# Half of the weights' low parts added up by DMA instead of subtracted on VectorE

## The chip, the cores and the metric

The kernel runs on one core of one Trainium2 chip. The metric is the device time of one execution in microseconds, lower is better. The kernel before takes 2055.74 us (median of 2 runs, 2055.71 to 2055.78).

## The reference

One decoder layer on 256 tokens of width 2048, everything in float32: a gated mixer (differential attention, a causal convolution, chunkwise retention), cross-attention into 256 memory tokens, a SwiGLU, and norms between them. Nearly all of the arithmetic is products of a 256-token activation with weight matrices:

```python
proj = h @ w_in                                   # 2048 x 13312
merged = g0*(ya @ w_branch[0]) + g1*(yb @ w_branch[1]) + g2*(yr @ w_branch[2])
x = x + merged @ w_out                            # 2048 x 2048
...                                               # cross-attention: wq, wkv, wo
x = x + (silu(a) * b) @ w2                        # a, b = split(h @ w13), hidden 5632
```

## The kernel before, in words

Every weight matrix is stored in chunks of 512 rows by 512 columns (1 MB, four k-tiles of 128 rows). A block is 512 output columns; for it the kernel runs through the chunks of the inner dimension. One chunk is loaded by one DMA from SyncE's queue into a tile `raw` of 8 KB a partition. SyncE's loads keep their program order (`ld`, line 71).

A chunk is worked on in two halves of two k-tiles (128 partitions x 1024 elements). The precision of float32 is kept by splitting both operands: the high part is the number rounded to float32r, the low part is the number minus the high part. For each half, `emit_split` lets ScalarE round `raw` into `wh` (line 161), and then lets VectorE write `wl` = `raw` - `wh` (line 162). `products` issues 12 matmuls for a half: for each of two k-tiles and two token tiles high x high (line 178), high x low (line 179), low x high (line 180).

The main stream is a list of halves, and `emit_half` issues the splits `LA` halves ahead of the products. `wh` and `wl` rotate through `hlp` (4 buffers of each), `raw` through `rawp` (5 buffers). A buffer is taken again when its last reader is done: a `wh` or a `wl` when TensorE has finished the half, a `raw` when both engines have split both of its halves. The remaining work (rotary embedding, convolution, attention, norms, transposes) is made of generators which are advanced by one step after each half (`pump`), so that it falls between the halves. The order on each engine is set by the scheduler, which works out times for all instructions while the program is built; loads on SyncE are exempt.

GpSimd has little to do: the power of -0.5 of a few norm statistics (line 230) and 16 loads of 512 KB outside the weights, from its own, software-driven DMA queue (decay, memtok, memT, xtok again, gfin: lines 535, 319, 243, 786, 938).

Line numbers from line 163 on are 4 higher in the changed kernel: what is line 180 before is line 184 there.

Of the kernel before, what the change touches and what calls it, by code (L numbers as in the profile page):

```python
# [24 lines left out]

# columns of the packed parameter tile
_PC = {}
# [12 lines left out]

LA = 3


class Act:
    """Four k-tiles of a transposed activation, as exact high and low float32r parts."""

# [7 lines left out]
def trunk(ctx, tc, xT, xtok, memT, memtok, w_in, w_br, w_out, w_q, w_kv, w_o, w_13, w_2,  # L54
          prm, cst, decay, gfin, out):
    nc = tc.nc
    P = 128

    cpool = ctx.enter_context(tc.tile_pool(name="cpool", bufs=1))
    rawp = ctx.enter_context(tc.tile_pool(name="rawp", bufs=5))  # L60
    hlp = ctx.enter_context(tc.tile_pool(name="hlp", bufs=4))
    s4 = ctx.enter_context(tc.tile_pool(name="s4", bufs=28))
# [27 lines left out]

    # ---------------------------------------------------------------- background tasks
    active = []
# [22 lines left out]

    # ---------------------------------------------------------------- main stream
    items = []
    halves = []

    def half_jobs(psref, chunks, acts, start, stop, alloc=None, ts=(0, 1), keep=False):  # L120
        """Products of activation chunks with weight chunks into the block's two banks."""
        n = len(chunks)
        for i, (w, a) in enumerate(zip(chunks, acts)):
            for h in range(2):
                j = dict(ps=psref, src=w, h=h, act=a, start=start and i == 0 and h == 0,
                         stop=stop and i == n - 1 and h == 1, alloc=alloc or alloc_mm, ts=ts, keep=keep)
                halves.append(j)
                items.append(("half", len(halves) - 1))
# [17 lines left out]
    def emit_split(i, before=None):  # L146
        j = halves[i]
        while state["dma"] <= i // 2:
            emit_dma(state["dma"])
        r = raws[i // 2]  # L150
        rv = r[:, 2 * j["h"]:2 * j["h"] + 2, :]
        if j["keep"]:
            hi = S4([P, 2, 512], F32R)
            lo = S4([P, 2, 512], F32R)
        else:
            hi = hlp.tile([P, 2, 512], F32R, tag="wh", name=nm("wh"))
            lo = hlp.tile([P, 2, 512], F32R, tag="wl", name=nm("wl"))
        for sl in ((slice(0, 1), slice(1, 2)) if i == 0 else (slice(0, 2),)):
            if before is not None:
                before(sl.start)  # L160
            sc.copy(hi[:, sl, :], rv[:, sl, :])  # L161
            ve.tensor_tensor(out=lo[:, sl, :], in0=rv[:, sl, :], in1=hi[:, sl, :].bitcast(F32), op=ALU.subtract)  # L162
        j["hi"], j["lo"] = hi, lo
        if j["h"] == 1:
            raws.pop(i // 2)
# [36 lines left out]
    def block(W, nb, acts, evac):  # L202
        """One 512-column block; evac(ps) is called once its products are issued."""
        ps = []
        half_jobs(ps, [W[nb, c] for c in range(len(acts))], acts, True, True)
        call(lambda: evac(ps[2]))

    # ---------------------------------------------------------------- constants
    prm_t = cpool.tile([P, PCOLS], F32, name="prm_t")
# [16 lines left out]
    def rstd_of(dst, src, scale, w):  # L226
        """dst = (src*scale + eps) ** -0.5 on a few columns."""
        v = TN(w)
        ve.tensor_scalar(out=v, in0=src, scalar1=scale, scalar2=EPS, op0=ALU.mult, op1=ALU.add)
        nc.gpsimd.tensor_tensor(out=dst, in0=v, in1=nhalf[:, :w], op=ALU.pow)  # L230
# [8 lines left out]
    def load_actT(a, src, g, c):  # L239
        """Load a transposed chunk, times its gain, in parts."""  # L240
        def gen():
            r = S4([P, 4, 256])
            nc.gpsimd.dma_start(out=r, in_=src[c])
            yield
            for k in range(0, 4, 2):
                actT_part(a, r, g, c, (k, k + 1))
                yield
        return gen()
# [6 lines left out]
    def transposed(a, src, gain):  # L255
        """Transposed chunk in parts: src(kt, t) are [128, 128] blocks; gain(kt) or None."""
        def gen():
            a.hi = S4([P, 4, 256], F32R)
            a.lo = S4([P, 4, 256], F32R)
            for pr in range(2):  # L260
                tp = TP().rearrange("p (k c) -> p k c", k=2)
                for k in range(2):
                    for t in range(2):
                        nc.tensor.transpose(tp[:, k, t * P:(t + 1) * P], src(2 * pr + k, t), ident)  # L264
                yield
                if gain is None:
                    sl = slice(2 * pr, 2 * pr + 2)
                    sc.copy(a.hi[:, sl, :], tp)  # L268
                    ve.tensor_tensor(out=a.lo[:, sl, :], in0=tp, in1=a.hi[:, sl, :].bitcast(F32),  # L269
                                     op=ALU.subtract)  # L270
                else:
                    for k in range(2):
                        split_gain(a, 2 * pr + k, tp[:, k, :], gain(2 * pr + k))
                yield
        return gen()

    def transposed_f32(dst, src):
        """dst [128, 4, 256] plain float32 transposes of src(kt, t)."""
        for pr in range(2):
# [8 lines left out]
    def blk(tl):  # L288
        """tl [128, 2, 512] token-major -> accessor of its [128,128] blocks."""
        return lambda k, t: tl[:, t, k * P:(k + 1) * P]  # L290

    def sumsq(tl, dst):
        """dst[:, t] = sum over the block's 512 columns of the square."""
        junk = S4([P, 2, 512])
        for t in range(2):
            sc.activation(junk[:, t, :], tl[:, t, :], AF.Square, accum_out=dst[:, t:t + 1])  # L296

    # ---------------------------------------------------------------- start
    gmix = cpool.tile([P, 16], F32, name="gmix")
# [14 lines left out]
    def tok_stats(src, dst, eng):  # L314
        """rstd of a token-major input."""
        parts = cpool.tile([P, 4, 2], F32, name=nm("parts"))
# [10 lines left out]
    def start_task():  # L327
# [24 lines left out]
        sc.activation(le, l2, AF.Exp)  # L352
        # -(e0 - e1 + lambda_init)
        ve.tensor_tensor(out=lam_t, in0=le[:, 1:2], in1=le[:, 0:1], op=ALU.subtract)
# [5 lines left out]
    def prologue():  # L360
        # keeps TensorE busy, and so at its full clock, while the first loads arrive
        sc.copy(warm, nhalf[:, 0:1])
# [20 lines left out]
    def scaled(ps, rs, extra=None):  # L383
        """Token-major copy of a block times the tokens' rstd."""
        o = S4([P, 2, 512])
# [3 lines left out]

    # ---------------------------------------------------------------- conv branch  # L390
    cv = {}
# [103 lines left out]

    # ---------------------------------------------------------------- rope
    def ev_rope(store, key, half, ro):
        """Rotary embedding on a block's heads, then its transposes."""
        nh = 512 // (2 * half)
# [25 lines left out]

    # ---------------------------------------------------------------- retention
    yr = [Act(), Act()]
# [65 lines left out]

    # ---------------------------------------------------------------- differential attention
    ya = [Act(), Act()]
# [88 lines left out]

    # ---------------------------------------------------------------- gated merge
    merged = [None] * 4
# [34 lines left out]

    # ---------------------------------------------------------------- keys and values of the memory
    kM = [None] * 4
# [25 lines left out]

    # ---------------------------------------------------------------- w_out, residual  # L750
    def residual(W, acts, xin, aT, gname, rs, parts, order=None):
        """x + acts @ W; the sum's rstd and its gained transposes for the next stage."""
        xs = [None] * 4
# [42 lines left out]

    # ---------------------------------------------------------------- cross-attention
    oT = [Act() for _ in range(4)]
# [14 lines left out]
    def prep_kv(h):  # L813
        """Parts of a head's transposed keys and of its values."""
        def gen():
# [12 lines left out]
    def mm3(out, l, r, start, stop):  # L828
        """out += l.T @ r from the parts (lhsT, rhs) of l and r."""
        nc.tensor.matmul(out, l[0], r[0], start=start, stop=False)  # L830
# [72 lines left out]

    # ---------------------------------------------------------------- SwiGLU
    hT = [Act() for _ in range(11)]
# [44 lines left out]
    def finish(nb, t, p):  # L950
        """Residual of one token tile's block; after the last one its norm and the store."""
        r = x2[nb][:, t, :]
# [137 lines left out]
```

## Time and profile before

| | before |
|---|---|
| median of the runs | 2055.74 us |
| span of the profiled execution, first to last instruction | 2054.3 us |
| TensorE busy | 2042.2 us, 99% |
| VectorE busy | 1194.7 us, 58% |
| ScalarE busy | 959.8 us, 47% |
| GpSimd busy | 20.3 us, 1% |
| bytes moved by DMA | 390.33 MB, 190 GB/s over the span |

The profile shows one execution. Busy time of an engine is time in which it executes an instruction; matmuls overlap in the pipeline, so that their summed durations are larger than TensorE's busy time. The page gives no time of the profiled execution besides its span; the median of the runs, which are timed without a profile, is 1.4 us longer than it. The chain of waits follows the end of the program back to its beginning: 99% of it is TensorE.

### The profile page before, as it was taken

The numbers are of one execution on the slowest core, as the hardware profiler recorded it, in microseconds if no ns is written. First come the engines' busy times: TensorE is split into PE (matmuls) and PEld (weight loads), VectorE is DVE, ScalarE is ACT, GpSimd is POOL, SyncE is SP. The second block draws the span as 40 slices with busy tenths as digits, with TensorE's granted clock in tenths as the row PEclk, the third lists the DMA queues.
The fourth block names the chain that finished last, engine by engine and source line by source line (L and its number), as shares of the span: only waits on it lengthen the run. The fifth ranks groups of instructions, "written<-read, shape, count | busy, mean of one in ns | idle before, by whom it ended". The sixth has DMA issues, their size and how long they took to land.

```text
span 2054.3 us, 23424 instructions
## 1 busy us (share of the span) xinstructions
PE 2042.2 (99%) x9369; PEld 1689.4 (82%) x9369; DVE 1194.7 (58%) x1505; ACT 959.8 (47%) x1190; POOL 20.3 (1%) x32
## 2 busy tenths in 40 slices
PE   9999999999999999999999999999999999999998
PEld 6888888888888888888888888888888888888886
DVE  6995699776654557444455555544455444455445
ACT  7444444558444455444445554444444334444443
POOL 0000000000000000000000000000000000000000
PEclk9999999999999999999999999999999999999999
DMA  9555444444555655655555444555555556555552
GB/s 374 185 188 202 174 175 174 166 164 163 186 212 196 220 200 215 227 203 185 200 186 182 151 149 158 184 185 188 196 189 184 189 200 207 195 192 185 185 199 88
DMA packets 57277, 390.33 MB, mean 190 GB/s; under 512 B 6480, under 2 KB 6736, under 8 KB 11984
## 3 DMA queue, kind: packets, MB, share of 16 engines
q1 hardware_dynamic: 54720, 380.44, 51.6%
q0 software_dynamic: 2304, 8.39, 1.1%
q8 instruction: 73, 1.20, 0.2%
q14 instruction: 36, 0.29, 0.0%
q10 hardware_dynamic: 144, 0.01, 0.0%
HBM read 386.72 MB, written 2.10 MB: 189 GB/s over the span
## 4 chain that ended last, share of the span: by engine, by line
PE 99%; DMA 0%; issue 0%; DVE 0%; SPq 0%; ACTq 0%; ACT 0%; POOLq 0%; POOL 0%
PE mm L178 31%; PE mm L179 31%; PE mm L180 31%; PE tp L264 1%; PE tp L178 1%; PE tp L179 1%; PE tp L180 1%; PE tp L283 0%; PE tp L832 0%; PE tp L831 0%; PE tp L830 0%; DMA raw<-in_w_in 0%; PE tp L622 0%; PE tp L558 0%; PE tp L620 0%
## 5 line engine op out<-in xcount | busy, mean ns | idle before, releaser
L162 DVE TENSOR_TENSOR wl<-raw,wh 128x1024 fp32r<-128x1024 f32 (+1 forms) x705 | 860.8, 1222 | 780.8 <-ACT wh L161 780.3
L161 ACT CAST wh<-raw 128x1024 fp32r<-128x1024 f32 (+1 forms) x705 | 740.8, 1052 | 956.2 <-PE mm L180 909.8
L178 PE MATMUL mm<-wh,s 128*128 128x512 f32 x2752 | 1078.4, 392 | 1.6 <-ACT wh L161 1.6
L179 PE MATMUL mm<-wl,s 128*128 128x512 f32 x2752 | 1075.3, 391 | 1.2 <-DVE wl L162 1.2
L180 PE MATMUL mm<-wh,s 128*128 128x512 f32 x2752 | 1073.7, 390 | 0.0
L178 PEld LDWEIGHTS mm<-wh,s 128*128 128x128 f32 x2752 | 516.8, 188 | 109.4 <-ACT wh L161 3.3
L180 PEld LDWEIGHTS mm<-wh,s 128*128 128x128 f32 x2752 | 516.7, 188 | 107.8
L179 PEld LDWEIGHTS mm<-wl,s 128*128 128x128 f32 x2752 | 517.0, 188 | 106.9 <-DVE wl L162 2.4
L433 DVE SCALAR_TENSOR_TENSOR s<-s,prm_t,s 128x227 f32<-128x227 f32 (+29 forms) x240 | 98.2, 464 | 0.0
L264 PE MATMUL tp<-cst_t,s 128*128 128x128 f32 x280 | 42.7, 272 | 0.0
L264 PEld LDWEIGHTS tp<-cst_t,s 128*128 128x128 f32 x280 | 34.5, 140 | 7.9
L269 DVE TENSOR_TENSOR s<-tp,s 128x512 fp32r<-128x512 f32 x46 | 31.1, 682 | 0.0
L251 ACT ACTIVATE s<-tp,prm_t 128x256 fp32r<-128x256 f32 x40 | 18.6, 472 | 19.1 <-DVE s L252 16.8
L268 ACT CAST s<-tp 128x512 fp32r<-128x512 f32 x46 | 26.4, 582 | 0.5 <-PE tp L264 0.5
L178 PE MATMUL tp<-wh,s 128*128 128x512 f32 x64 | 24.9, 389 | 0.0
L179 PE MATMUL tp<-wl,s 128*128 128x512 f32 x64 | 24.9, 389 | 0.0
L180 PE MATMUL tp<-wh,s 128*128 128x512 f32 x64 | 24.9, 389 | 0.0
L252 DVE SCALAR_TENSOR_TENSOR s<-tp,prm_t,s 128x256 fp32r<-128x256 f32 x40 | 19.0, 480 | 9.1 <-ACT s L251 9.1
L913 ACT ACTIVATE s<-mm,rs 128x512 f32<-128x512 f32 x22 | 13.9, 686 | 16.7 <-PE mm L180 16.7
L694 ACT ACTIVATE s<-mm,rsx 128x512 f32<-128x512 f32 x24 | 15.2, 685 | 12.5 <-PE mm L180 12.4
L296 ACT ACTIVATE s<-s 128x512 f32<-128x512 f32 x32 | 19.9, 624 | 1.4 <-DVE s L758 1.4
L921 DVE SCALAR_TENSOR_TENSOR s<-mm,rs,s 128x512 f32<-128x512 f32 x22 | 15.5, 747 | 4.6 <-PE mm L180 4.6
(172 smaller groups left out, 682.2 us busy)
## 6 DMA issues: line engine op xcount, KB each, us to landing
raw<-in_w SPq DMA_DIRECT2D x132, 1024.0 KB, 4.8
raw<-in_w_in SPq DMA_DIRECT2D x117, 1024.0 KB, 4.8
raw<-in_w_kv SPq DMA_DIRECT2D x32, 1024.0 KB, 4.8
raw<-in_w_br SPq DMA_DIRECT2D x24, 1024.0 KB, 4.8
raw<-in_w_out SPq DMA_DIRECT2D x16, 1024.0 KB, 4.8
raw<-in_w_q SPq DMA_DIRECT2D x16, 1024.0 KB, 4.9
raw<-in_w_o SPq DMA_DIRECT2D x16, 1024.0 KB, 4.8
raw<-in_w_in SPq DMA_DIRECT2D x5, 512.0 KB, 9.3
```

What stands on the lines that cost most here:

```text
L161: sc.copy(hi[:, sl, :], rv[:, sl, :])
L162: ve.tensor_tensor(out=lo[:, sl, :], in0=rv[:, sl, :], in1=hi[:, sl, :].bitcast(F32), op=ALU.subtract)
L178: nc.tensor.matmul(ps[t], ah, hi[:, k, :], start=j["start"] and k == 0, stop=False)
L179: nc.tensor.matmul(ps[t], ah, lo[:, k, :], start=False, stop=False)
L180: nc.tensor.matmul(ps[t], al, hi[:, k, :], start=False, stop=stop and k == 1)
L251: sc.activation(a.hi[:, k, :], src, AF.Identity, scale=g)
L252: ve.scalar_tensor_tensor(out=a.lo[:, k, :], in0=src, scalar=g, in1=a.hi[:, k, :].bitcast(F32), op0=ALU.mult, op1=ALU.subtract)
L264: nc.tensor.transpose(tp[:, k, t * P:(t + 1) * P], src(2 * pr + k, t), ident)
L268: sc.copy(a.hi[:, sl, :], tp)
L269: ve.tensor_tensor(out=a.lo[:, sl, :], in0=tp, in1=a.hi[:, sl, :].bitcast(F32), op=ALU.subtract)
L296: sc.activation(junk[:, t, :], tl[:, t, :], AF.Square, accum_out=dst[:, t:t + 1])
L433: ve.scalar_tensor_tensor(out=o[:, s:], in0=uT[:, k, :T - s], scalar=pc("cw", c * CW + CW - 1 - s), in1=o[:, s:], op0=ALU.mult, op1=ALU.add)
```

## The change

Of each chunk from the fifth on (`i >= 8`), the second half gets its low part in another way. ScalarE rounds `raw` a second time, with the sign turned, straight into `wl`; a DMA from GpSimd's queue then reads the same weights from HBM once more and adds them to `wl` in SBUF. The first half of each chunk, the first four chunks and the last weights (`keep`) are split as before. The look-ahead goes from 3 halves to 4, `hlp` from 4 to 5 buffers, `rawp` from 5 to 4. The other lines of the diff drop comments and are left out here.

```diff
-LA = 3
+LA = 4
...
-    rawp = ctx.enter_context(tc.tile_pool(name="rawp", bufs=5))
-    hlp = ctx.enter_context(tc.tile_pool(name="hlp", bufs=4))
+    rawp = ctx.enter_context(tc.tile_pool(name="rawp", bufs=4))
+    hlp = ctx.enter_context(tc.tile_pool(name="hlp", bufs=5))
...
             sc.copy(hi[:, sl, :], rv[:, sl, :])
+            if i >= 8 and i % 2 == 1 and not j["keep"]:
+                sc.activation(lo, rv, AF.Identity, scale=-1.0)
+                nc.gpsimd.dma_start(out=lo, in_=j["src"][:, 2:4, :], accum_op=ALU.add)
+                continue
             ve.tensor_tensor(out=lo[:, sl, :], in0=rv[:, sl, :], in1=hi[:, sl, :].bitcast(F32), op=ALU.subtract)
```

In the whole program 348 half-chunks are changed: ScalarE has 348 instructions more (line 163), VectorE 348 fewer, GpSimd 348 DMAs more (line 164).

ScalarE in the input projection, before (`raw` is a chunk, `wh` the high part of a half):

```order
L161 CAST wh_767<-raw_765 128x1024
L161 CAST wh_785<-raw_765 128x1024
L161 CAST wh_805<-raw_803 128x1024
L161 CAST wh_825<-raw_803 128x1024
L161 CAST wh_846<-raw_844 128x1024
```

and in the changed kernel:

```order
L161 CAST wh_726<-raw_724 128x1024
L163 ACTIVATE wl_745<-raw_724 128x1024
L161 CAST wh_744<-raw_724 128x1024
L161 CAST wh_765<-raw_763 128x1024
L163 ACTIVATE wl_784<-raw_763 128x1024
L161 CAST wh_783<-raw_763 128x1024
```

Three instructions per chunk stand where two were, and the scheduler puts the negated copy of the second half ahead of that half's own rounding.

GpSimd at the second retention group, before (`tn` are statistics of a norm, `s` from `in_decay` is a load):

```order
L230 TENSOR_TENSOR rsx<-tn_428,nhalf 128x2
L535 DMA s_201_1333<-in_decay 128x1024
L230 TENSOR_TENSOR tn_1923<-tn_1924,nhalf 128x8
L535 DMA s_332_2112<-in_decay 128x1024
L230 TENSOR_TENSOR tn_2700<-tn_2701,nhalf 128x8
```

and in the changed kernel, the stretch that ends with the same second load:

```order
L164 DMA wl_1802<-in_w_in 128x1024
L164 DMA wl_1849<-in_w_in 128x1024
L234 TENSOR_TENSOR tn_1967<-tn_1968,nhalf 128x8
L164 DMA wl_1902<-in_w_in 128x1024
L164 DMA wl_1972<-in_w_in 128x1024
L164 DMA wl_2034<-in_w_in 128x1024
L164 DMA wl_2083<-in_w_in 128x1024
L164 DMA wl_2138<-in_w_in 128x1024
L539 DMA s_334_2158<-in_decay 128x1024
```

The powers of the norms and the loads, which had this queue to themselves, now stand between the adding DMAs.

## Rows read from the trace of the kernel before

**Rows 1.** The page's first part: engine, busy us (share of the span) xinstructions.

```profile
PE 2042.2 (99%) x9369; PEld 1689.4 (82%) x9369; DVE 1194.7 (58%) x1505; ACT 959.8 (47%) x1190; POOL 20.3 (1%) x32
```

**Rows 2.** Waits, last SyncE's queue: engine line <- waited for: us, times, longest us.

```profile
ACT wh L161 <- PE mm L180: 909.8, 574, 6.1
...
PE mm L178 <- ACT wh L161: 1.6, 3, 0.5
...
SPq L71 <- DVE wl L162: 1730.3, 329, 12.3
```

**Rows 3.** Timeline, 900 to 903 us: start us, us, engine, instruction [idle before <-releaser].

```profile
901.40 0.39 PE L180 MATMUL mm<-wh,s 128*128 128x512 f32 x1
...
901.63 0.39 PE L178 MATMUL mm<-wh,s 128*128 128x512 f32 x1
...
901.83 1.05 ACT L161 CAST wh<-raw 128x1024 fp32r<-128x1024 f32 x1 [1.67 <-PE mm L180]
901.85 0.39 PE L179 MATMUL mm<-wl,s 128*128 128x512 f32 x1
```

**Rows 4.** ScalarE's timeline over the end of a block, same columns.

```profile
1733.98 1.05 ACT L161 CAST wh<-raw 128x1024 fp32r<-128x1024 f32 x1 [1.67 <-PE mm L180]
1736.70 1.27 ACT L913 ACTIVATE s<-mm,rs 128x512 f32<-128x512 f32 x2 [1.67 <-PE mm L180]
1737.86 1.05 ACT L161 CAST wh<-raw 128x1024 fp32r<-128x1024 f32 x1
1739.42 1.05 ACT L161 CAST wh<-raw 128x1024 fp32r<-128x1024 f32 x1 [0.52 <-PE mm L180]
```

**Rows 5.** Groups by form: line engine op xcount | busy us, mean ns | idle before.

```profile
L162 DVE TENSOR_TENSOR wl<-raw,wh 128x1024 fp32r<-128x1024 f32 x703 | 859.4, 1224 | 777.8 <-ACT wh L161 777.3
L161 ACT CAST wh<-raw 128x1024 fp32r<-128x1024 f32 x703 | 739.5, 1053 | 953.2 <-PE mm L180 909.8 <-PE tp L180 13.5 <-DVE s L433 10.0
...
L913 ACT ACTIVATE s<-mm,rs 128x512 f32<-128x512 f32 x22 | 13.9, 686 | 16.7 <-PE mm L180 16.7
```

**Rows 6.** DMA queues: packets, MB, share of 16 engines; issues: KB, us to landing.

```profile
q1 hardware_dynamic: 54720, 380.44, 51.6%
q0 software_dynamic: 2304, 8.39, 1.1%
...
raw<-in_w SPq DMA_DIRECT2D x132, 1024.0 KB, 4.8
...
s<-in_memT POOLq DMA_DIRECT2D x4, 512.0 KB, 4.6
```

**Rows 7.** GpSimd's loads of `memT`, all four: time from issue to landing.

```profile
DMA to landing us min/median/max: 3.9/4.6/4.9
```

**Rows 8.** GpSimd's load of `decay` at 40.6 us: time from issue to landing.

```profile
DMA to landing us min/median/max: 9.1/9.1/9.1
```

**Rows 9.** Stretches: us, busy us of each engine, granted clock, DMA share, GB/s.

```profile
25.00:50.00 25.00, 25.00 (x112) 20.71 (x111) 14.21 (x24) 18.06 (x27) 1.35 (x2) 1.00 1.01 417
50.00:200.00 150.00, 150.00 (x679) 124.40 (x679) 121.01 (x200) 66.16 (x69) 0.00 (x0) 1.00 0.54 191
200.00:600.00 400.00, 400.00 (x1912) 329.74 (x1911) 295.10 (x535) 204.96 (x294) 8.50 (x7) 1.00 0.49 176
600.00:900.00 300.00, 300.00 (x1341) 248.79 (x1340) 162.76 (x151) 141.61 (x169) 6.51 (x12) 1.00 0.59 209
900.00:1000.00 100.00, 100.00 (x442) 82.78 (x442) 45.33 (x37) 44.12 (x48) 0.00 (x0) 1.00 0.54 191
1000.00:1400.00 400.00, 400.00 (x1928) 335.25 (x1927) 215.29 (x236) 196.03 (x267) 1.41 (x2) 1.00 0.49 175
1400.00:2000.00 600.00, 600.00 (x2686) 496.11 (x2684) 295.53 (x261) 249.65 (x256) 1.10 (x2) 1.00 0.54 192
```

**Rows 10.** GpSimd's timeline, three of its rows.

```profile
231.90 1.67 POOL L230 TENSOR_TENSOR tn<-tn,nhalf 128x8 f32<-128x8 f32 x1 [190.60 <-DVE tn L229]
...
769.32 1.10 POOL L243 DMA_DIRECT2D s<-in_memT  x2
...
841.13 1.05 POOL L786 DMA_DIRECT2D s<-in_xtok  x2 [61.45 <-PE mm L180]
```

## The prediction

> **What bounds the kernel now.** I read the page's first part, then who waited for whom, then a short timeline, then the DMA tables. TensorE is busy for 99% of the span, VectorE for 58%, ScalarE for 47% [rows 1]. The waits say which of them sets the pace: ScalarE's rounding waits 909.8 us for TensorE to give buffers back, TensorE waits 1.6 us for ScalarE, and SyncE's queue waits 1730.3 us for VectorE to free a `raw` [rows 2]. So everything runs ahead of TensorE and is held back by buffers; nothing but TensorE's own pace is on the path. That pace can be read off ScalarE's clockwork: a rounding every 2.72 us (1733.98, 1736.70), with 1.67 us of idle time ended by TensorE [rows 4]. A half has 12 matmuls, so one is issued every 0.227 us, and a chunk takes 5.44 us. TensorE idles 2054.3 - 2042.2 = 12 us in all, which is the most that any change off TensorE can give back: 0.6%.
>
> **What is removed.** 348 subtractions of 1.224 us on VectorE [rows 5], 426 us: VectorE goes from 1194.7 to about 769 us, 37%. Since TensorE did not wait for it, this is worth nothing.
>
> **What ScalarE gets.** 348 negated roundings of 128x1024 from SBUF. Their form is not in the trace. From below it is the rounding of the same shape, 1.05 us; from above two scaled activations of 128x512 from PSUM, 2 x 0.686 = 1.37 us [rows 5]. I take 1.2 us, between them: 418 us, so that ScalarE stands at 1378 us, 67%. In each chunk it has 2 x 1.05 + 1.2 = 3.3 us of 5.44, which leaves 2.1 us for the rest. At a block's end the eviction pushes a rounding back by 1737.86 - 1736.70 = 1.16 us, and the one after it is on time again [rows 4]. A block ends with a second half; with 5 buffers, what is freed then goes to a first half, so the pushed one is not the negated copy. I put ScalarE at nothing; its cover is the spare time below.
>
> **What the low part now waits for.** This is the term that decides. Before, three halves of lead are 8.2 us, of which rounding and subtraction take 2.3: 5.9 us to spare. Now the negated copy for half i starts when TensorE leaves half i-5. The timeline has that distance: the last matmul of a half starts at 901.40, the next half at 901.63, the freed rounding at 901.83, so 0.20 us into the half [rows 3]. `wl` is first read by the second matmul of half i, 0.23 us into it. From one to the other are 4 x 2.72 + 0.23 - 0.20 = 10.9 us; less 1.2 for the copy, **9.7 us are left for the adding DMA from issue to landing**.
>
> No adding DMA is in the trace. From below it is a plain load of the same 512 KB from the same queue: 3.9 us at the least, 4.6 at the median [rows 7]. From above I take two of the slowest in a row, one to read the weights and one to read what they are added to: 4.9 + 4.9 = 9.8 us. I choose 4.6 us and one more reading of 0.52 MB at the best rate shown, 417 GB/s [rows 9], 1.26 us: 5.9 us, because the additional half is a stream and not a second round from issue to landing. That leaves 3.8 us to spare, and no steady wait. If a landing takes L all the time, the four halves stretch until they hold it: each chunk grows by (L - 9.7) / 2, and 348 chunks by 174 us for each microsecond too many.
>
> **What the DMA engines get.** 348 x 0.524 MB = 182 MB beside 390 MB. A `raw` of 1.05 MB takes 2.5 us at 417 GB/s. With each added byte read once, a chunk needs 2.5 + 1.26 = 3.8 us of 5.44; with the destination read as well, 2.5 + 2.5 = 5.0 us. Both fit at that rate. The loads of `raw` keep their cover: a `raw` is freed about 2.5 us into half 2k-3, and the chunk that takes it, four later, is wanted at half 2k+4, so 7 x 2.72 - 2.5 = 16.5 us for a load that lands in 4.8 [rows 6]. One buffer fewer of `raw` therefore costs nothing, as long as the engines are not full.
>
> The Trainium skill's Collectives: The Full Stack (The bandwidth ceiling: the fold count and why AG ≠ RS ≠ AR) says that a reduction by DMA is half as fast as a copy, not because of the add but because both sources are read through the same ring. By that rule the second of the two figures holds, 5.0 us of 5.44, and my sum stays as it is, with little room; no row here has an adding DMA to test it.
>
> **Where small losses are.** (1) The start. From 25 to 50 us the DMA engines are full, 417 GB/s at a share of 1.01 [rows 9], and a 512 KB load issued there landed after 9.1 us [rows 8]. Five adding DMAs fall there (halves 9 to 17, from 26 us on, every 5.44 us). 9.1 + 1.26 = 10.4 us is 0.7 late, half of that per chunk: 2 us. They also bring 2.6 to 5.2 MB, 6 to 12.6 us of full engines, most of which displaces loads that are not urgent. I take 5 us in all, from 0 to 15. (2) GpSimd's queue. Its issues take 0.53 us (1.10 for two) and the powers 1.67 us [rows 10]; either fits into 3.8 us. The queue is in order, though: an adding DMA behind a power waits as long as that power waits for VectorE's statistics, and the four loads of `xtok` now stand in a row ahead of one, 4 x 1.26 = 5.0 us of transfer, 1.2 us too many. I take 3 us, from 0 to 40 (some 20 places at up to 2 us).
>
> **The sum.** -0 (VectorE) + 0 (ScalarE) + 5 (start) + 3 (GpSimd's queue) = +8 us on the profiled span of 2054.3; the median of the runs is 1.4 us above that span, so 2055.74 + 8 = **2064 us**. Its own range is 2050 to 2096: TensorE's idle time cannot give back more than a few us, and the upper end is that of GpSimd's queue, 40 us.
>
> **The rivals.** *The DMA engines are full.* For it: the share of busy engines, as the profile counts it, is much higher than the best rate suggests: 0.54 at 191 or 192 GB/s [rows 9]. If that share is work and not waiting, and an adding DMA costs two readings, then each byte of `raw` brings another of the same cost. Adding up the stretches in which the doubled share passes 1: 50 to 200 us 1.08, +12; 600 to 900 us, where 0.05 of the 0.59 are other loads, 1.13, +38; 900 to 1000, 1.08, +8; 1400 to 2000, 1.08, +48; the stretches with 0.49 stay under 1. Together 106 us and the 8 from above: 2170. If it costs three plain readings at 417 GB/s, a chunk takes 2.5 + 3.8 = 6.3 us against 5.67 (348 chunks in about 1975 us): +219, 2283. At four, 7.5 us and some 2720. It decides from 5.67 - 2.5 = 3.2 us of all 16 engines per adding DMA. Against it: 417 GB/s held for 25 us. Chance 0.33. The rule of the skill named above is this rival's two readings.
>
> *The landing is late, with engines to spare.* Reading, adding and writing back in turn, behind the other queue's packets, could take longer than 9.7 us everywhere. If the start's 10.4 us became the rule: 0.7 x 174 = 122 us, 2186; at 11 us, 2290. For it: 9.1 us has been seen for a plain load. Against it: only where the engines were full; 3.9 to 4.9 elsewhere. Chance 0.15. This one and the one before end on the slower side.
>
> *GpSimd's queue holds the adding DMAs up* at each power and load, 40 us: about 2100. Chance 0.05; against it speaks that VectorE, whose statistics are waited for, gets freer.
>
> *Faster by what VectorE gives up.* TensorE's idle time is 12 us in all [rows 1], far from 2%, so that it would have to issue its matmuls closer than every 0.227 us, for which nothing speaks. Chance 0.01.
>
> **How the numbers follow.** The forecast keeps 0.46: it is the likeliest single case, though the slower ones together hold more. A difference under about 2% is what two measurements of this kernel would call none (2015 to 2097 us). Faster 0.01, within 2% 0.46, slower 0.53 (0.33 + 0.15 + 0.05). The range goes from 2050 to 2350: it takes in the forecast, the full engines at two and three readings, late landings to about 11 us and the queue; what is left out is four readings and more, and later landings, some 0.2.
>
> **What would show it.** If right: TensorE's waits for `wl` stay at a few us outside the first 60 us, the adding DMAs land in 5 to 8 us, the DMA share is 0.75 to 0.95, ScalarE still waits for TensorE. If the engines are full: a share near 1 all along, `raw` landing much later than 4.8 us, ScalarE waiting for `raw`. If the landing is late: TensorE waiting at line 183 (the old 179) for the DMA once in each chunk, with a share well under 1. If the queue: long gaps on GpSimd ended by VectorE just before an adding DMA. My price of the adding DMA is the weakest step; all else rests on rows.

## The result, and the profile after

| | before | changed |
|---|---|---|
| median of the runs, 2 of each | 2055.74 us | 2135.8 us |
| ratio, with its 95% interval | | 1.0389 (1.0358 to 1.0419) |
| span of the profiled execution | 2054.3 us | 2136.0 us |

The change costs 80 us, 3.9%. The forecast of 2064 us was the likeliest single case and did not come; the time lies in the range, on the slower side that held 0.53.

The page's first part of the changed kernel, to be read against [rows 1]:

```profile
PE 2073.7 (97%) x9369; PEld 1688.4 (79%) x9369; DVE 781.1 (37%) x1157; ACT 1280.8 (60%) x1536; POOL 322.7 (15%) x380
```

VectorE moved about as worked out (769 us were expected), ScalarE by less (1378). TensorE has the same 9369 matmuls, but is idle for 62 us instead of 12, and busy for 31 us more: a matmul lasts 0.39 us and the next one starts after 0.23, so that a short wait between them shows no idle time, and a matmul that waits for its weights only a little shows as a longer one.

Who waited for whom, all engines (columns as in [rows 2]; line 183 is the old 179):

```profile
ACT wl L163 <- PE mm L183: 380.4, 294, 10.1
...
PEld mm L183 <- DMA wl<-in_w: 29.7, 35, 3.2
...
PE mm L183 <- DMA wl<-in_w: 15.5, 23, 2.8
...
PE mm L183 <- DMA wl<-in_w_out: 6.8, 1, 6.8
```

TensorE now waits at the matmul that first reads `wl`, and for a DMA. ScalarE still waits for TensorE, so it isn't the bound. The DMA part of the page, against [rows 6]:

```profile
q0 software_dynamic: 52416, 190.86, 49.5%
q1 hardware_dynamic: 54720, 380.44, 46.8%
...
raw<-in_w SPq DMA_DIRECT2D x132, 1024.0 KB, 9.5
...
wl<-in_w POOLq DMA_DIRECT2D x128, 512.0 KB, 10.0
```

Both queues together take 96% of the engines' time by the profile's count; before it was 53%. A `raw` lands after 9.5 us instead of 4.8. The adding DMAs (line 164), all 348:

```profile
DMA to landing us min/median/max: 5.5/9.8/19.4
```

The timeline around two of them (columns as in [rows 3]):

```profile
1497.67 0.87 POOL L164 DMA_DIRECT2D wl<-in_w  x1 [4.81 <-ACT wl L163]
...
1501.93 1.06 ACT L163 ACTIVATE wl<-raw 128x1024 fp32r<-128x1024 f32 x1 [1.40 <-PE mm L183]
1501.96 0.39 PE L182 MATMUL mm<-wh,s 128*128 128x512 f32 x1
...
1503.29 0.87 POOL L164 DMA_DIRECT2D wl<-in_w  x1 [4.75 <-ACT wl L163]
...
1503.95 0.33 SPq L71 DMA_DIRECT2D raw<-in_w  x1
...
1507.40 0.39 PE L182 MATMUL mm<-wh,s 128*128 128x512 f32 x1
1507.76 0.19 PEld L183 LDWEIGHTS mm<-wl,s 128*128 128x128 f32 x1 [0.39 <-DMA wl<-in_w]
1507.76 0.50 PE L183 MATMUL mm<-wl,s 128*128 128x512 f32 x1
```

Two things are to be seen. The first matmul on `wl` (1507.76) starts 0.36 us after the one before it, where 0.23 is the pace. It waits for the adding DMA of 1497.67, some 10 us before, which is late by a hair. This does not happen in every chunk. From 1400 to 2000 us, inside the SwiGLU, 105 adding DMAs are issued, and the waits of TensorE's weight loads for them in that stretch are 29 (us, times, longest us):

```profile
PEld mm L183 <- DMA wl<-in_w: 22.3, 29, 1.5
```

And the load of the next `raw` is issued 0.66 us after the adding DMA (1503.95 against 1503.29), so that the two share the engines nearly from beginning to end. Four stretches, against [rows 9]:

```profile
25.00:50.00 25.00, 23.23 (x103) 18.91 (x102) 5.35 (x7) 19.52 (x33) 4.34 (x5) 1.00 1.03 350
...
200.00:600.00 400.00, 398.50 (x1904) 327.10 (x1903) 221.23 (x471) 262.53 (x358) 65.41 (x71) 1.00 0.95 259
600.00:900.00 300.00, 288.20 (x1260) 233.01 (x1259) 93.03 (x93) 180.30 (x213) 49.27 (x61) 0.99 1.00 283
...
1400.00:2000.00 600.00, 588.25 (x2597) 476.93 (x2595) 159.27 (x149) 341.22 (x356) 91.87 (x107) 1.00 1.00 277
```

The number behind TensorE's busy time counts its matmuls. Where it has much other work between the chunks (200 to 600 us) it issues 1904 instead of 1912, next to no loss; from 600 to 900 us 1260 instead of 1341; in the SwiGLU (1400 to 2000 us) 2597 instead of 2686, 3.3% or 20 us. The granted clock is the same in the SwiGLU, so the loss there is waiting.

The longest wait stands where four loads of `xtok` go ahead of an adding DMA in GpSimd's queue:

```profile
1052.75 2.47 POOL L790 DMA_DIRECT2D s<-in_xtok  x4
1057.66 0.88 POOL L164 DMA_DIRECT2D wl<-in_w_out  x1 [2.44 <-ACT wl L163]
```

TensorE idles for 6.8 us, until 1077.1, and around the end of this wait its granted clock is at about half, the lower of its two levels (1.2 instead of 2.4 GHz):

```profile
1074.00:1081.00 7.00, 3.85 (x9) 3.09 (x10) 0.00 (x0) 0.00 (x0) 0.00 (x0) 0.51 0.94 246
```

Over the whole run the mean granted clock is 0.994, against 0.999 before. An estimate from these two: 0.005 x 2136 = 11 us at the most, of the 80, are clock lost with the long waits.

### The profile page after: what moved, and what is told of

It is laid out like the page before. It is cut to its first block, busy times and chain, and to the rows that moved or that the text cites. A ratio compares the mean times of both kernels' runs of the same rounds, so it can differ in the third digit from the quotient of the medians.

```text
span 2136.0 us, 24639 instructions
## 1 busy us (share of the span) xinstructions
PE 2073.7 (97%) x9369; PEld 1688.4 (79%) x9369; DVE 781.1 (37%) x1157; ACT 1280.8 (60%) x1536; POOL 322.7 (15%) x380
## 3 DMA queue, kind: packets, MB, share of 16 engines
q0 software_dynamic: 52416, 190.86, 49.5%
## 4 chain that ended last, share of the span: by engine, by line
issue 49%; PE 33%; POOL 9%; DMA 8%; ACT 1%; DVE 0%; POOLq 0%; SPq 0%; ACTq 0%
PE mm L183 10%; PE mm L182 10%; PE mm L184 10%; POOL wl L164 8%; DMA wl<-in_w_in 3%; DMA wl<-in_w_br 2%; DMA wl<-in_w_out 1%; DMA wl<-in_w 1%; PE tp L268 1%; DMA wl<-in_w_kv 0%; DMA wl<-in_w_o 0%; ACT wl L163 0%; DMA raw<-in_w_in 0%; PE tp L836 0%; PE tp L835 0%
## 5 line engine op out<-in xcount | busy, mean ns | idle before, releaser
L183 PE MATMUL mm<-wl,s 128*128 128x512 f32 x2752 | 1086.9, 395 | 46.9 <-DMA wl<-in_w 15.5
L166 DVE TENSOR_TENSOR wl<-raw,wh 128x1024 fp32r<-128x1024 f32 (+1 forms) x357 | 435.7, 1221 | 1038.0 <-ACT wh L161 1037.5
L163 ACT ACTIVATE wl<-raw 128x1024 fp32r<-128x1024 f32 x348 | 368.9, 1060 | 390.4 <-PE mm L183 380.4
L164 POOL DMA_DIRECT2D wl<-in_w x128 | 110.7, 864 | 622.8 <-ACT wl L163 605.5
L164 POOL DMA_DIRECT2D wl<-in_w_in x116 | 100.9, 870 | 586.6 <-ACT wl L163 532.6
L437 DVE SCALAR_TENSOR_TENSOR s<-s,prm_t,s 128x255 f32<-128x255 f32 (+29 forms) x240 | 94.6, 462 | 0.0
L164 POOL DMA_DIRECT2D wl<-in_w_kv x32 | 27.6, 863 | 152.7 <-ACT wl L163 147.4
L164 POOL DMA_DIRECT2D wl<-in_w_br x24 | 20.8, 867 | 113.9 <-ACT wl L163 106.9
L164 POOL DMA_DIRECT2D wl<-in_w_o x16 | 13.8, 864 | 93.9 <-ACT wl L163 73.3
L164 POOL DMA_DIRECT2D wl<-in_w_q x16 | 13.9, 866 | 85.3 <-ACT wl L163 79.1
```

The costliest lines, as they stand in the source:

```text
L163: sc.activation(lo, rv, AF.Identity, scale=-1.0)
L164: nc.gpsimd.dma_start(out=lo, in_=j["src"][:, 2:4, :], accum_op=ALU.add)
L183: nc.tensor.matmul(ps[t], ah, lo[:, k, :], start=False, stop=False)
L437: ve.scalar_tensor_tensor(out=o[:, s:], in0=uT[:, k, :T - s], scalar=pc("cw", c * CW + CW - 1 - s), in1=o[:, s:], op0=ALU.mult, op1=ALU.add)
```

## The experiments

Two theories stood after the result. **T1**: the DMA engines are full, and the chunk takes as long as its bytes. **T2**: the engines have time left, but the low part lands later than the buffers' lead allows.

**The adding DMA left out.**

```diff
                 sc.activation(lo, rv, AF.Identity, scale=-1.0)
-                nc.gpsimd.dma_start(out=lo, in_=j["src"][:, 2:4, :], accum_op=ALU.add)
                 continue
```

> The adding DMA is left out (so the second halves' low parts are only the negated rounded copy); ScalarE's third instruction per chunk, the longer look-ahead and the other buffer counts stay. Both theories (T1: the DMA engines are full; T2: the engines have time, but the low part lands later than the buffers' lead of about 9.5 us from issue) put the whole loss on the adding DMA: 2050 to 2062 us, DMA share 0.5. If ScalarE's 348 copies or the buffers cost something, the time stays above 2070.

Measured: 2055.93 us, ratio 1.0001 (0.9991 to 1.0010). Its engines:

```profile
PE 2042.6 (99%) x9369; PEld 1689.4 (82%) x9369; DVE 780.7 (38%) x1157; ACT 1282.8 (62%) x1536; POOL 21.1 (1%) x32
```

ScalarE's 348 instructions, VectorE's 414 us less, the look-ahead and the buffers are together worth nothing. All of the loss belongs to the DMA.

**A plain load in its place.**

```diff
-                nc.gpsimd.dma_start(out=lo, in_=j["src"][:, 2:4, :], accum_op=ALU.add)
+                nc.gpsimd.dma_start(out=lo, in_=j["src"][:, 2:4, :])
```

> The same DMA from the same queue and of the same 512 KB, but a plain load that overwrites the copy (the addition is left out). T1: the engines' time per second half goes from 2.97 to about 1.4 us, a chunk needs 4.3 us of 5.67, no wait: 2056 to 2065 us, DMA share near 0.78, landing 5 to 7 us. T2 with the second reading as the cause of the lateness: the same time. If it is GpSimd's queue or the sharing of the engines by two queues that makes it late, and not the addition: 2100 us and more, landing over 9 us.

Measured: 2062.29 us, ratio 1.0028 (1.0015 to 1.0041). Its queues and the landing of the 348 loads:

```profile
q1 hardware_dynamic: 54720, 380.44, 45.4%
q0 software_dynamic: 52416, 190.86, 34.8%
```

```profile
DMA to landing us min/median/max: 4.1/6.2/13.2
```

The same number of DMAs and the same bytes from HBM through the same queue cost 6 us. So nearly all of the loss is the addition's, and not the queue's. By the packets' time a plain DMA takes (34.8% - 1.2%) x 2061.7 / 348 = 1.99 us of all engines, an adding one (49.5% - 1.2%) x 2136.0 / 348 = 2.96 us (1.2% is the share of the queue's other loads, from the run without the DMA).

**Every half by adding DMA.** With two adding DMAs in each chunk, the most that the engines can do should show.

```diff
-            if i >= 8 and i % 2 == 1 and not j["keep"]:
+            if i >= 8 and not j["keep"]:
...
-                nc.gpsimd.dma_start(out=lo, in_=j["src"][:, 2:4, :], accum_op=ALU.add)
+                nc.gpsimd.dma_start(out=lo, in_=j["src"][:, 2 * j["h"]:2 * j["h"] + 2, :], accum_op=ALU.add)
```

> Every half from the ninth on gets its low part by the adding DMA. T1: a chunk then needs 2.75 + 2 x 2.97 = 8.7 us of the DMA engines: about 3050 to 3150 us, share near 1. T2: the engines still fit, each half is late by some us of the four halves' lead: 2200 to 2450 us.

Measured, in a single run: 2727.13 us, between the two expectations. A stretch of the SwiGLU, which comes later in this longer run:

```profile
2000.00:2500.00 500.00, 406.54 (x1630) 295.06 (x1629) 18.40 (x24) 277.32 (x288) 115.23 (x133) 0.99 1.05 280
```

A chunk moves 1.05 MB of `raw` and as much by adding, 2.10 MB at 280 GB/s: 7.49 us. If an adding DMA reads both of its sources, 3.15 MB are read in that time, 420 GB/s, which is about the best rate of the kernel before, 417 [rows 9]. So an adding DMA of 0.52 MB costs the engines as much as a plain load of 1.05 MB, 2.5 us, and not the 2.96 that its packets' time gave in the changed kernel. The changed kernel then needs 2 x 2.5 = 5.0 us of 5.44 (2.96 was waiting in part): 92%. T1 is not right as it stands, but there is little room. The second reading is inferred from this agreement of rates alone: the profile counts the same packets and bytes for an adding DMA as for a plain one, and that the pace of this run is the engines' and not that of GpSimd's queue was not shown in another way.

**One half more of lead.** The copy and its DMA for the second half are issued with the first half's split, into a sixth buffer.

```diff
+        if i >= 8 and i % 2 == 0 and not j["keep"]:
+            l2 = early[i + 1] = hlp.tile([P, 2, 512], F32R, tag="wl", name=nm("wl"), bufs=6)
+            sc.activation(l2, r[:, 2:4, :], AF.Identity, scale=-1.0)
+            nc.gpsimd.dma_start(out=l2, in_=j["src"][:, 2:4, :], accum_op=ALU.add)
```

> The negated copy and its adding DMA are issued one half earlier (wl has 6 buffers, one tile less in the pool of the background work), so the lead grows by 2.72 us, to about 12.2 us from issue to landing. T1: the engines have no more time than before, so that the queue only gets longer: 2120 to 2140 us, landing 11 us and more. T2: the 9.8 us now fit, TensorE waits no more: 2056 to 2070 us.

Measured: 2087.02 us, ratio 1.0156 (1.0139 to 1.0173), between the two again: three fifths of the loss are gone, which full engines would not have given back, but not all of it. In the SwiGLU it issues 2652 matmuls of 2686, and the landing is not longer than in the changed kernel. The lead grew by less than was expected. Counted off in the trace, from the issue of an adding DMA in the SwiGLU to the first matmul that reads its `wl`, it is 11.3 us at the median, against 9.8 for the changed kernel (worked out in the next section): 1.5 us more and not 2.72.

```profile
1400.00:2000.00 600.00, 596.34 (x2652) 491.42 (x2652) 161.73 (x151) 348.69 (x362) 94.41 (x110) 0.99 1.00 283
```

```profile
DMA to landing us min/median/max: 5.4/9.1/16.7
```

From this came **T3**, a sharper T2: the engines are some 90% used; the adding DMA is late because it shares them with a load of `raw` that is issued at the same time and is not urgent.

**Two halves more of lead.** As before, but issued with the second half's split of the chunk before (7 buffers of `wl`; the tables of the rotary embedding move into a tile of the background work to make room).

```diff
+        if i >= 9 and i % 2 == 1 and i + 2 < len(halves) and not halves[i + 2]["keep"]:
...
+            l2 = early[i + 2] = hlp.tile([P, 2, 512], F32R, tag="wl", name=nm("wl"), bufs=7)
+            sc.activation(l2, raws[i // 2 + 1][:, 2:4, :], AF.Identity, scale=-1.0)
+            nc.gpsimd.dma_start(out=l2, in_=halves[i + 2]["src"][:, 2:4, :], accum_op=ALU.add)
```

> The negated copy and its adding DMA are issued two halves earlier than in the changed kernel (7 buffers of wl, paid by one tile of the background work and by tables moved into such a tile): about 15 us from issue to landing. T3: waits only at the start, 2056 to 2070 us, with the landing still at 8.5 to 10 us. T1: no better than the 2087 us of one half more.

Measured: 2062.53 us, ratio 1.0035 (1.0023 to 1.0046).

```profile
1400.00:2000.00 600.00, 600.00 (x2686) 496.29 (x2685) 163.37 (x153) 351.57 (x364) 94.80 (x111) 1.00 1.01 287
```

```profile
PE mm L190 <- DMA wl<-in_w_out: 4.3, 1, 4.3
```

```profile
DMA to landing us min/median/max: 5.4/9.0/20.4
```

This is the run that decides. The lead, counted in the same way, is 16.7 us. In the SwiGLU each chunk moves the same bytes and the share is 1.01; the landing takes 9.0 us, little less than the 9.8 of the changed kernel; and there is not one matmul fewer than in the kernel before. The engines were not full there; the lead was too short. The one long wait that is left (line 190 here is line 183 of the changed kernel) is the one behind the loads of `xtok`.

**The adding DMA on the first half.** As many and as large, with the same lead, but away from the load of `raw`.

```diff
-            if i >= 8 and i % 2 == 1 and not j["keep"]:
+            if i >= 8 and i % 2 == 0 and not j["keep"]:
...
-                nc.gpsimd.dma_start(out=lo, in_=j["src"][:, 2:4, :], accum_op=ALU.add)
+                nc.gpsimd.dma_start(out=lo, in_=j["src"][:, 0:2, :], accum_op=ALU.add)
```

> The adding DMA makes the low part of every first half instead of every second one: as many, as large, with the same lead. But the buffer of raw is then given back one half later, by the second half's split, so that the next load of raw is issued about 3.5 us after the adding DMA and not 0.66 us after it. T3 (the engines are about 90% used and not full; the adding DMA is late because it shares them with a load of raw that was issued at the same time and is not urgent): it lands after 6.5 to 8.5 us, 2056 to 2075 us. T1 (the engines are full): the bytes are the same, 2120 to 2140 us.

Measured: 2097.77 us, ratio 1.0202 (1.0186 to 1.0217): half of the loss is gone, less than T3 expected. Its timeline has the load of `raw` 4.0 us behind the adding DMA, and the landing is 1.4 us shorter than in the changed kernel:

```profile
1500.75 0.87 POOL L164 DMA_DIRECT2D wl<-in_w  x1 [4.57 <-ACT wl L163]
...
1504.73 5.82 SPq L71 DMA_DIRECT2D raw<-in_w  x2
...
1506.19 0.87 POOL L164 DMA_DIRECT2D wl<-in_w  x1 [4.57 <-ACT wl L163]
```

```profile
DMA to landing us min/median/max: 5.4/8.4/16.2
```

```profile
1400.00:2000.00 600.00, 596.73 (x2659) 491.37 (x2658) 164.38 (x153) 347.12 (x364) 94.12 (x110) 1.00 1.01 283
```

In the SwiGLU 27 matmuls are missing instead of 89, so the part that T3 speaks of shrank by more than two thirds. The sharing is a cause of the lateness, then, but moving one load does not end it: the load still meets the next adding DMA, which is issued 1.46 us behind it. Of the remaining 42 us, one wait of 6.4 us stands where the four loads of `xtok` go ahead in GpSimd's queue. Matmuls are also missing at the start (80 instead of 112 from 25 to 50 us, where a wait of 4.6 us ends and the mean granted clock is 0.86), from 600 to 900 us (1296 instead of 1341) and from 1000 to 1400 us (1884 instead of 1928); these were not taken apart.

**Half the bytes, as many DMAs.**

```diff
-                sc.activation(lo, rv, AF.Identity, scale=-1.0)
-                nc.gpsimd.dma_start(out=lo, in_=j["src"][:, 2:4, :], accum_op=ALU.add)
+                sc.activation(lo[:, 1:2, :], rv[:, 1:2, :], AF.Identity, scale=-1.0)
+                nc.gpsimd.dma_start(out=lo[:, 1:2, :], in_=j["src"][:, 3:4, :], accum_op=ALU.add)
+                ve.tensor_tensor(out=lo[:, 0:1, :], in0=rv[:, 0:1, :], in1=hi[:, 0:1, :].bitcast(F32), op=ALU.subtract)
```

> As many adding DMAs, each of 256 KB: the other k-tile of the half is subtracted on VectorE. T3 and T1: a chunk needs 2.6 + 1.3 = 3.9 us of the engines, the DMA lands after 6 to 8 us: 2056 to 2066 us. If a fixed cost of each adding DMA made it late, and not its bytes: above 2100 us.

Measured: 2061.22 us, ratio 1.0035 (1.0023 to 1.0048).

```profile
DMA to landing us min/median/max: 4.1/6.3/12.6
```

As expected: a fixed cost of an adding DMA is not what makes it late.

**Half as many DMAs, the same size.**

```diff
-            if i >= 8 and i % 2 == 1 and not j["keep"]:
+            if i >= 8 and i % 4 == 1 and not j["keep"]:
```

> Only every fourth half-chunk (the second half of every second chunk) gets its low part by the adding DMA: the bytes of the run before with half as many DMAs. T3: each adding DMA still meets a load of raw, and lands after 8 to 9.5 us, at the edge of the lead: 2058 to 2080 us. T1: the engines need 2.6 + 1.3 us in a chunk on the mean: 2056 to 2062 us.

Measured: 2071.52 us, ratio 1.0076 (1.0061 to 1.0091).

```profile
DMA to landing us min/median/max: 5.5/8.3/11.7
```

The same bytes as in the run before cost 10 us more. Each adding DMA still meets a load of `raw` and lands 2 us later than the small one, as T3 expected. But 8.3 us lie inside the lead of 9.8, and the SwiGLU loses nothing; the cost lies in a few waits elsewhere:

```profile
PE mm L183 <- DMA wl<-in_w_in: 5.0, 3, 2.6
PE mm L183 <- DMA wl<-in_w_br: 4.1, 1, 4.1
```

```profile
1400.00:2000.00 600.00, 600.00 (x2686) 496.16 (x2685) 228.57 (x207) 299.88 (x310) 48.34 (x57) 1.00 0.83 239
```

One of these four waits is at the start. The other three are for adding DMAs issued between 772 and 801 us, only some 4 to 7 us ahead of where TensorE would have read their `wl`. So the longer landing costs where the lead is short, and the 10 us do not speak for T3 in each chunk.

No version beats the kernel before, and none could by much: without the adding DMA TensorE is at 99% in 2055.93 us.

## Why the prediction was right and wrong

- **What bounds the kernel, and the gain of nothing**: right. 414 us fewer on VectorE changed the time by 0.01% (-0.09 to +0.10).
- **ScalarE at nothing**: right. Its copy takes 1.06 us, at the lower bound and not the 1.2 chosen, and the run without the DMA shows the cover to be enough. ScalarE was busy for 1280.8 us, not 1378.
- **The lead**: right, in part by luck. I put the copy 0.20 us into a half, where a freed `wh` is rounded. But a `wl` has its last reader one matmul earlier, and the copy starts at 1501.93, before the half does (1501.96). It takes 1.06 us and not 1.2, and GpSimd issues 0.30 us behind its end, at 1503.29, which I had left out. That leaves 1501.96 + 4 x 2.72 + 0.23 - 1503.29 = 9.8 us, against 9.7. (The expectations of the runs went by about 9.5.)
- **The start**: 5 us were forecast. From 25 to 50 us 103 matmuls stand for 112, 2 us; but the lateness does not end there (from 50 to 200 us 641 for 679).
- **The landing**: this is the step that failed. I took 5.9 us, a plain load of 4.6 us and one more reading at the best rate; it measured 9.8 at the median. That this is the upper bound of 4.9 + 4.9 is chance: the bound stood for two loads in a row, and one plain load in the same place lands after 6.2. The 1.3 us for the second reading were about right: the shortest landing is 5.5 us, against 4.1 for a plain load, 0.33 of it longer issuing. What was left out is that the median of 4.6 belongs to engines that are half used. With the adding DMAs they are used to nine tenths, each adding DMA lies beside a whole load of `raw`, and both take the time of both: 2.5 + 2.5 us of transfer instead of 1.26 + 1.26. By these numbers an estimate is 4.6 - 1.26 + 5.0 = 8.3 us, which is what it took where only every second chunk had an adding DMA (8.3). The other 1.5 us were not taken apart.
- **The price of being late**: right in kind, wrong in size. With the lead of 9.8 us the formula, (L - 9.8) / 2 x 348, gives nothing for a median of 9.8, and 80 us were lost. It has one landing time for all, but the landings run from 5.5 to 19.4 us, and TensorE waits for each one that is later than its lead, in the longest waits at the cost of its clock as well. A lead of 11.3 us took back 49 us, one of 16.7 took back 73.
- **The rivals.** "The landing is late, with engines to spare", held at 0.15, is what happened, at a smaller lateness than either of its prices (2186, 2290). "The engines are full", held at 0.33 with 2170 for two readings, came nearer in time and had two of the three signs that I named for it, a share near 1 and `raw` landing later. The third was missing: ScalarE waited for `raw` for 9.3 us in all. And with two halves more of lead no matmul was lost in the SwiGLU at the same share. So the share was a false sign, also for the other rival, which I had given "a share well under 1": it is the time that packets are under way, and it stood at 1.01 with room left. By rate the room was there, as the sum had it: 5.0 us of 5.44. The range held the time because it was drawn for the rivals too; the forecast's own, 2050 to 2096, did not.
- **The rule weighed there** (the Trainium skill, Collectives: The Full Stack, The bandwidth ceiling: the fold count and why AG ≠ RS ≠ AR): the trace agrees, as far as rates can tell. With every half added, the engines read 420 GB/s if both sources are counted, against 417 for plain loads.
- **GpSimd's queue**: the 3 us were too few. Issuing an adding DMA takes 0.86 us against 0.53 for a plain one, which mattered little, but behind the four loads of `xtok` TensorE waits once for 6.8 us, and even with two halves more of lead for 4.3.

## What to carry to other kernels

A transfer's landing time is read at the load of the moment; when a change adds traffic, ask first what else will be issued beside it, and add that transfer's time too. A wait of this kind is set against the lead in buffers, not against bandwidth, and the lead is set against the late landings, not the median: here both were 9.8 us, and 3.9% were lost. Before engines are called full, their rate is compared with the best the trace shows, and more buffers tell the two apart; how much lead they really gave is counted off in the trace. Where an urgent DMA and one that is not urgent are issued together, look whether one of them can move: here they shared the engines, and the urgent one paid.

## What the runs showed of the hardware

An adding DMA into SBUF cost the DMA engines about as much as a plain load of twice its size (an estimate of 2.5 us for 0.52 MB, from 420 GB/s of readings if both sources are counted). At the least it landed 1.4 us later than a plain one (5.5 against 4.1 us), and GpSimd took 0.86 us instead of 0.53 to issue it. The share of busy engines stood at 1.00 to 1.01 at 277 as well as at 287 GB/s (second readings not counted), and it was 1.01 at 417 GB/s in the kernel before [rows 9]. Around the end of a wait of 6.8 us TensorE's mean granted clock was 0.51 (1074 to 1081 us).
